# Reordering the last groups of a hybrid decoder layer: projections of p, the turn of x1, and the buffers of split weights

## The chip, the cores and the metric

The kernel runs on one core of a Trainium2 chip. The metric is the device time of one execution in microseconds; the time before is the median of three runs. A profiled execution beside them gives the trace: every instruction of the five engines (TensorE is PE, its weight loads PEld, VectorE is DVE, ScalarE is ACT, GpSimdE is POOL) and the transfers that SyncE (SP) and ACT issue.

## The reference, cut to what matters

One layer with 256 tokens and a width of 2048. All arithmetic is float32.

```python
h = rmsnorm(x, norm_mix_g)
u = h @ w_in                       # 2048 x 12288, ten fields
ya = b * causal_dwconv3(c * xa, conv_w) * silu(za)
yb = rmsnorm_per_head(hgrn2(silu(q), f, iv)) * hg_norm_g * silu(og)
m = sigmoid(ga) * (ya @ w_a_out) + sigmoid(gb) * (yb @ w_b_out)
x = x + m @ w_o                    # this x is called x1 below
gate = sigmoid(rmsnorm(x, ple_norm_g) @ w_ple_gate)
x = x + gate * (p @ w_ple_proj)    # p is 256 x 256
out = rmsnorm(x, final_norm_g)
```

The change concerns the last four lines.

## The kernel before

**Products.** Each float32 operand is split into a high and a low part, and each product is three matmuls: high with high, high with low, low with high (`product`, L834 to L836). The stationary operand is a slice of 128 tokens by 128 features, the moving one 512 columns of weights. A weight matrix is cut into *groups* of 512 output columns, and a group into *chunks* of 256 input features. A chunk is 12 matmuls: two slices of 128 features, two halves of the tokens, three products. Each group fills two PSUM banks, one for each half of the tokens.

**The order of the groups** is the list `groups`: 24 of w_in with those of w_a and w_b between them, then O0 to O3 (w_o, eight chunks each), then PP0, PG0, PP1, PG1, PP2, PG2, PP3, PG3. PP is the projection of p (w_pp, one chunk), PG the gate (w_pg, eight chunks). Chunk c of PG needs features 256 c to 256 c + 255 of x1, so chunks 6 and 7 of each PG group need the quarter that O3 makes. PG3 is written apart, after the loop: it runs over its eight chunks three times (first half of the tokens with 512 columns, then the second half with 256 columns, twice), keeps its eight split pairs throughout, and its results go straight into the final norm.

**Weights** come in loads of two chunks (1 MB; those of w_pp have one chunk) into three raw buffers, issued by SP in order (`load`, L105; w_pp at L103). `split` (L118 and L119) makes a pair of each chunk: ACT copies the high part `whi`, DVE subtracts and writes the low part `wlo`. Pairs up to the second chunk of PG3 take four buffers in turn; the last six chunks of PG3 have six buffers of their own, in the pool `late`, which is opened at PP0 in the place of m. A pair's buffer is free when PE has done its chunk, a raw buffer when DVE has split both of its chunks. `ahead` says how far ahead of PE's chunk splits are written: three chunks, rising to eight over the first chunks of PG2:

```python
return LEAD + min(max(pos - (last_group - 8), 0), 5)
```

**Epilogues** are generators: each `advance()`, once for every chunk, runs the next piece of each that is active. `step` ties a piece behind the latest split on ACT and on DVE (`issue_after`). A scheduler then orders each engine's instructions from what is written and from its own estimates; on the chip every engine works through its list in that order. The epilogues that matter here:

- `ep_o` (after O0 to O3): DVE adds the two banks to x (L584), ACT squares for the norm (L585) and copies into another order (L591), then `turned` writes to DRAM with four transfers (L191) and reads back with one (L193), and after a lag of three pieces DVE transposes (L197). `put` then makes the high part `xh` on ACT (L155) and the low part `xl` on DVE (L156), four pieces each.
- `ep_pp` (after PP): ACT copies the two banks to `pw` (L608).
- `ep_pg` (after PG0 to PG2): ACT's sigmoid reads the two banks (L618), DVE multiplies by `pw` and adds to x (L621, L622), ACT squares (L623), POOL multiplies by the final gain (L630).

**PSUM.** The groups' banks are four, given in turn, so a group's two banks are those of the group before last; PG3 takes one bank for each of its three passes. PE can start a group only when the readers of the banks' earlier contents are done.

Of the kernel before, what the change touches and what calls it, by code (L numbers as in the profile page):

```python
# [11 lines left out]
AF = mybir.ActivationFunctionType  # L12
# [5 lines left out]
NT = T // P  # L18
# [5 lines left out]
CW = 512  # L24
# [20 lines left out]
def hybrid_kernel(ctx, tc, xT, x, pT, prm, gfin, masks, w_in, w_a, w_b, w_o, w_pg, w_pp, out):  # L45
    nc = tc.nc

    const = ctx.enter_context(tc.tile_pool(name="const", bufs=1))
    wp = ctx.enter_context(tc.tile_pool(name="wp", bufs=1))
# [6 lines left out]
    pools, closers = {}, {}  # L56

    def open_pool(name, side):
        closers[name] = ExitStack()
        pools[name] = closers[name].enter_context(  # L60
            tc.tile_pool(name=name, bufs=1, side=side, reuse_waits="tile")
        )

    def close_pool(name):
        closers.pop(name).close()
        del pools[name]
# [3 lines left out]
    state = {"tmp": "tmp1"}  # L70
# [3 lines left out]
    def nm(s):  # L74
        uid[0] += 1
        return f"{s}_{uid[0]}"

    def t4(tag="t4", bufs=None):
        bufs = bufs or {"tmp1": 8, "tmp2": 5, "tmp3": 5}[state["tmp"]]
        return pools[state["tmp"]].tile([P, 1024], F32, tag=tag, bufs=bufs, name=nm(tag))  # L80
# [4 lines left out]
    def sc(n, tag="sc", bufs=12):  # L85
        return small.tile([P, n], F32, tag=tag, bufs=bufs, name=nm(tag))
# [21 lines left out]
    def split(pos, halves=(0, 1)):  # L108
        w, g, c = stream[pos]
        src = load(pos)[:, c % 2, :]  # L110
        pool, n = (pools["late"], 6) if pos >= last_group + 2 else (wp, 4)
        if pos not in parts:
            parts[pos] = tuple(
                pool.tile([P, 2 * CW], F32R, tag=tag, bufs=n, name=nm(tag)) for tag in ("whi", "wlo")
            )
        hi, lo = parts[pos]
        s = slice(halves[0] * CW, (halves[-1] + 1) * CW)
        a = nc.scalar.activation(out=hi[:, s], in_=src[:, s], func=AF.Copy)  # L118
        v = nc.vector.tensor_tensor(  # L119
            out=lo[:, s], in0=src[:, s], in1=hi[:, s].bitcast(F32), op=ALU.subtract  # L120
        )
        state["splits"] = (a.ins, v.ins)
# [18 lines left out]
    def gain(base, k):  # L141
        return prm_t[:, base + k : base + k + 1]
# [28 lines left out]
    def blocks(ap):  # L171

        return ap.rearrange("p (c b e) -> p c b e", b=4, e=32)

    def spread(ap, t):

        return ap.rearrange("p (b c t e) -> p t c b e", b=4, c=4, t=NT)[:, t]  # L180

    def turned(src, lag, dst=None):

        d = dram.tile([P, 4, T], F32, tag="turn", bufs=3, name=nm("turn"))
        to = d.rearrange("(b i) a x -> a i b x", b=4)
        for a in range(4):  # L190
            nc.sync.dma_start(out=to[a], in_=src[32 * a : 32 * a + 32, :].rearrange("i (b x) -> i b x", b=4))  # L191
        yield
        nc.sync.dma_start(out=src, in_=d.rearrange("p a x -> p (a x)"))  # L193
        for _ in range(lag):
            yield
        dst = t4() if dst is None else dst
        nc.vector.transpose(  # L197
            out=dst.rearrange("p (k a e) -> p a k e", a=4, e=32), in_=src.rearrange("p (a k e) -> p a k e", a=4, e=32)
        )
        return dst  # L200
# [377 lines left out]

    def ep_o(j, psum):
        xs = state["x"]  # L580
        src = t4()
        for t in range(NT):
            d = xs[:, t, j * CW : (j + 1) * CW]
            nc.vector.tensor_tensor(out=d, in0=d, in1=psum[t], op=ALU.add)  # L584
            nc.scalar.activation(  # L585
                out=src[:, t * CW : (t + 1) * CW], in_=d, func=AF.Square,
                accum_out=state["ss2"][:, t * 4 + j : t * 4 + j + 1],
            )
        x1 = src
        for t in range(NT):  # L590
            nc.scalar.activation(  # L591
                out=spread(x1, t), in_=blocks(xs[:, t, j * CW : (j + 1) * CW]), func=AF.Copy
            )
        x1 = yield from turned(x1, 3)
        for c in range(4):
            put(state["x1T"], j * 4 + c, x1[:, c * T : (c + 1) * T], gain(PRM_GPLE, j * 4 + c))
        if j == 3:
            tot = sc(2, "tot2", 1)
            nc.vector.tensor_reduce(
                out=tot, in_=state["ss2"].rearrange("p (t j) -> p t j", t=NT),  # L600
                axis=mybir.AxisListType.X, op=ALU.add,
            )
            state["rstd2"] = rsqrt_of(tot, NT, D, "r2")
# [76 lines left out]
    groups = []  # L680
    for n, (kind, j) in enumerate(IN_ORDER):
        groups.append((kind, j, w_in, n, "hT"))
        if kind == "gb":
            groups.append(("A", j, w_a, j, "yaT"))
            groups.append(("B", j, w_b, j, "ybT"))
    groups += [("O", j, w_o, j, "mT") for j in range(4)]
    for j in range(4):
        groups.append(("PP", j, w_pp, j, "pT"))
        groups.append(("PG", j, w_pg, j, "x1T"))
    steps = []  # L690
    for gi, (kind, j, w, g, op) in enumerate(groups):
        for c in range(w.shape[2]):
            stream.append((w, g, c))
            steps.append((gi, c))

    last_group = len(steps) - w_pg.shape[2]
# [3 lines left out]
    LEAD, AHEAD = 3, 4  # L700
# [3 lines left out]
    for c in range(KT // 2):  # L704
        n = 2 * (c % 2)
        nc.sync.dma_start(
            out=xraw[c // 2].rearrange("p (k t) -> p k t", k=4)[:, n : n + 2, :],
            in_=xT[:, 2 * c : 2 * c + 2, :],
# [14 lines left out]
    def put_x(k):  # L723
        put(state["hT"], k, xraw[k // 4][:, (k % 4) * T : (k % 4 + 1) * T], gain(PRM_GMIX, k))
# [82 lines left out]
        state["ss3"] = sc(12, "ss3", 1)  # L807
        nc.gpsimd.memset(state["ss3"].rearrange("p (t j) -> p t j", t=NT)[:, :, 5:6], EPS)

    def step(e):  # L810

        a, v = state["splits"]
        with tc.issue_after(a), tc.issue_after(v):
            try:
                next(e)
            except StopIteration:
                active.remove(e)

    def advance():
        for e in list(active):  # L820
            step(e)

    def finish():
        while active:
            advance()

    def ahead(pos):

        return LEAD + min(max(pos - (last_group - 8), 0), 5)

    def product(psum, op, k, t, hi, lo, first, last):

# [2 lines left out]
        nc.tensor.matmul(psum, oh, lo, start=False, stop=False)  # L835
        nc.tensor.matmul(psum, ol, hi, start=False, stop=last)  # L836

    active = []
    psum = None
    done = 0  # L840
    for pos, (gi, c) in enumerate(steps[:last_group]):
        kind, j, w, g, opname = groups[gi]
        nch = w.shape[2]
        if kind == "PP" and j == 0:
            close_pool("m")
            open_pool("late", "left")
        while done < min(pos + 1 + ahead(pos), len(steps)):
            if done < 2:
                for i in range(2):
                    put_x(2 * done + i)  # L850
                    split(done, (i,))
            else:
                for k in range(2 * done, min(2 * done + 2, KT)):
                    put_x(k)
                split(done)
            done += 1
        if pos == 4:
            begin()
        if 0 <= pos - NORM < 4:
            add_squares(pos - NORM)  # L860
        if pos == NORM + 3:
            norm_of_x()
        if pos == NORM + 4:
            active.append(ep_f(0, waiting))
            step(active[-1])
            nc.sync.dma_start(out=mask_t, in_=masks)
        if c == 0:
            psum = [bank("g") for _ in range(NT)]
        hi, lo = parts.pop(pos)
        for i in range(2):  # L870
            k = 2 * c + i
            s = slice(i * CW, (i + 1) * CW)
            for t in range(NT):
                product(psum[t], state[opname], k, t, hi[:, s], lo[:, s], k == 0, k == 2 * nch - 1)

        for q in range(done, min(done + AHEAD, len(steps)) if pos >= FIRST else 0):
            load(q)
        if 0 <= pos - TOKENS < 4:
            load_tokens(pos - TOKENS)
        advance()  # L880
        if kind == "O" and j == 0 and c == nch - 3:
            finish()
            third_part()
        if kind == "O" and j > 0 and c == 1:
            residual(j)
        if kind == "O" and j in (1, 2) and c == 4:
            (load_p, load_gfin)[j - 1]()
        if c == nch - 1:
            if kind == "f" and j == 0:

                waiting = psum
                for n in ("yaT", "ybT"):
                    state[n] = operand(pools["branch"], n, DC // P)
            if kind == "ga" and j == 0:
                finish()
                second_part()
            if kind == "O" and j == 0:
                state["x1T"] = operand(big, "x", KT)
            if kind == "f" and j == 0:
                continue  # L900
            active.append(epilogues[kind](j, psum))
            step(active[-1])

# [1 line left out]
    for t, halves in ((0, (0, 1)), (1, (0,)), (1, (1,))):  # L907
        bk, n = bank("g"), CW // 2
# [91 lines left out]
```

## Time and profile before

| | before |
|---|---|
| median of 3 runs | 842.76 us (842.6 to 843.79) |
| profiled execution | 842.37 us |
| its span | 840.6 us |
| PE busy | 824.0 us, 98% of the span |
| DVE busy | 528.3 us, 63% |
| ACT busy | 435.4 us, 52% |
| mean granted TensorE clock | 0.995 |

The span runs from the first instruction of the program to the last; the execution's own time is 1.8 us longer. Matmuls overlap, each row of one lasting longer than the step to the next, so the step from start to start is what a matmul costs. A bracket at the end of a row gives the idle time of that engine before it, and who ended it.

### The profile page before, as it was taken

What the parts mean: (1) busy time and instruction counts of PE and PEld (TensorE: products, weight loads), DVE (VectorE), ACT (ScalarE), POOL (GpSimd) and SP (SyncE); (2) the same over time, 40 slices, a digit from 0 to 9 for tenths busy, and PEclk for the clock granted to TensorE, in tenths of its full rate; (3) what the DMA queues carried; (4) which work ended last, traced back from release to release, by engine and by line L of the source; (5) the groups of instructions that cost most, each with busy time, mean ns of one, the idle gap of its engine ahead of it and who ended that gap; (6) DMA issues with size and microseconds to landing.
All of it is one profiled execution on the core that took longest, in us unless ns stands there. A gap on an engine that the chain in (4) does not pass through costs nothing.

```text
span 840.6 us, 9805 instructions
## 1 busy us (share of the span) xinstructions
PE 824.0 (98%) x3752; PEld 683.3 (81%) x3752; DVE 528.3 (63%) x600; ACT 435.4 (52%) x563; POOL 91.5 (11%) x76
## 2 busy tenths in 40 slices
PE   8999999999999999999999999999999999999985
PEld 5888888888888888888888888888888888878865
DVE  7558687777674777877546446454555566655552
ACT  7566654545564654545544444444444555654543
POOL 1000153100000243100001001001001000002110
PEclk9999999999999999999999999999999999999998
DMA  9977555648775555458557557556556877865512
GB/s 335 367 252 254 181 195 176 225 151 288 254 234 187 191 198 190 161 197 283 188 191 244 200 200 241 191 191 228 204 197 225 292 261 255 305 225 177 205 70 101
DMA packets 39792, 183.01 MB, mean 218 GB/s; under 512 B 4544, under 2 KB 13760, under 8 KB 21824
## 3 DMA queue, kind: packets, MB, share of 16 engines
q1 hardware_dynamic: 39312, 181.81, 62.4%
q8 instruction: 29, 0.48, 0.2%
q10 hardware_dynamic: 432, 0.56, 0.2%
q14 instruction: 19, 0.16, 0.0%
HBM read 170.82 MB, written 11.53 MB: 217 GB/s over the span
## 4 chain that ended last, share of the span: by engine, by line
PE 94%; DMA 2%; issue 1%; ACT 1%; DVE 1%; SPq 0%; POOLq 0%; POOL 0%
PE g L836 31%; PE g L835 31%; PE g L834 31%; PE s L327 1%; DMA raw<-in_w_pg 1%; DMA raw<-in_w_in 1%; ACT whi L118 1%; DVE wlo L119 1%; PE s L436 0%; PE s L449 0%; PE s L448 0%; PE s L447 0%; ACT xs L659 0%; ACT t L642 0%; SPq L713 0%
## 5 line engine op out<-in xcount | busy, mean ns | idle before, releaser
L119 DVE TENSOR_TENSOR wlo<-raw,whi 128x1024 fp32r<-128x1024 f32 (+1 forms) x294 | 360.2, 1229 | 272.4 <-ACT whi L118 271.7
L118 ACT ACTIVATE whi<-raw 128x1024 fp32r<-128x1024 f32 (+1 forms) x294 | 308.9, 1053 | 353.2 <-PE g L836 314.2
L834 PE MATMUL g<-whi,xh 128*128 128x512 f32 (+1 forms) x912 | 352.9, 388 | 6.2 <-ACT t L618 3.4
L835 PE MATMUL g<-wlo,xh 128*128 128x512 f32 (+1 forms) x912 | 352.6, 387 | 0.0
L836 PE MATMUL g<-whi,xl 128*128 128x512 f32 (+1 forms) x912 | 352.0, 386 | 0.0
L834 PEld LDWEIGHTS g<-whi,xh 128*128 128x128 f32 x912 | 171.6, 188 | 42.0 <-ACT t L618 3.9
L835 PEld LDWEIGHTS g<-wlo,xh 128*128 128x128 f32 x912 | 171.7, 188 | 34.9 <-DVE wlo L119 1.2
L836 PEld LDWEIGHTS g<-whi,xl 128*128 128x128 f32 x912 | 171.7, 188 | 34.9 <-DVE xl L156 0.5
L835 PE MATMUL g<-wlo,mh 128*128 128x512 f32 x128 | 49.6, 389 | 0.0
L834 PE MATMUL g<-whi,mh 128*128 128x512 f32 x128 | 49.5, 389 | 0.0
L836 PE MATMUL g<-whi,ml 128*128 128x512 f32 x128 | 49.5, 389 | 0.0
L572 POOL TENSOR_TENSOR t<-ga,gb 128x512 f32<-128x512 f32 x8 | 14.1, 1789 | 249.1 <-DVE gb L568 249.1
L836 PEld LDWEIGHTS g<-whi,ml 128*128 128x128 f32 x128 | 24.0, 188 | 5.0
L834 PEld LDWEIGHTS g<-whi,mh 128*128 128x128 f32 x128 | 24.0, 188 | 5.0
L835 PEld LDWEIGHTS g<-wlo,mh 128*128 128x128 f32 x128 | 24.0, 188 | 4.9
L373 POOL TENSOR_TENSOR t<-b 128x512 f32<-128x512 f32 x10 | 20.8, 2085 | 65.3 <-DMA raw<-in_w_in 33.6
L355 POOL TENSOR_TENSOR X<-t,kT 128x256 f32<-128x256 f32 x12 | 14.1, 1173 | 99.4 <-ACT t L369 57.7
L834 PE MATMUL g<-whi,yaTh 128*128 128x512 f32 x64 | 24.9, 389 | 0.0
L835 PE MATMUL g<-wlo,yaTh 128*128 128x512 f32 x64 | 24.9, 389 | 0.0
L836 PE MATMUL g<-whi,yaTl 128*128 128x512 f32 x64 | 24.9, 389 | 0.0
L834 PE MATMUL g<-whi,ybTh 128*128 128x512 f32 x64 | 24.9, 389 | 0.0
L835 PE MATMUL g<-wlo,ybTh 128*128 128x512 f32 x64 | 24.9, 389 | 0.0
(148 smaller groups left out, 555.5 us busy)
## 6 DMA issues: line engine op xcount, KB each, us to landing
raw<-in_w_in SPq DMA_DIRECT2D x91, 1024.0 KB, 4.9
raw<-in_w_o SPq DMA_DIRECT2D x16, 1024.0 KB, 5.9
raw<-in_w_pg SPq DMA_DIRECT2D x16, 1024.0 KB, 4.8
turn<-t SPq DMA_DIRECT2D x72, 128.0 KB, 2.9
t<-turn SPq DMA_DIRECT2D x18, 512.0 KB, 4.9
raw<-in_w_a SPq DMA_DIRECT2D x8, 1024.0 KB, 4.9
raw<-in_w_b SPq DMA_DIRECT2D x8, 1024.0 KB, 5.0
raw<-in_w_in SPq DMA_DIRECT2D x9, 512.0 KB, 7.7
```

Source lines behind the costliest of these rows:

```text
L118: a = nc.scalar.activation(out=hi[:, s], in_=src[:, s], func=AF.Copy)
L119: v = nc.vector.tensor_tensor(out=lo[:, s], in0=src[:, s], in1=hi[:, s].bitcast(F32), op=ALU.subtract)
L327: nc.tensor.matmul(bk[:, s], X[:, 0, h, :], X[:, 1, h, :], start=True, stop=True)
L355: eng.tensor_tensor(out=xv[:, w, :, :, half, :], in0=ev[:, :, blk, :, half, :], in1=src[:, :, blk, :, half, :], op=ALU.mult,)
L373: nc.gpsimd.tensor_tensor(out=er, in0=br, in1=ref, op=ALU.subtract)
L572: nc.gpsimd.tensor_tensor(out=spread(m, t), in0=blocks(ga[:, s]), in1=blocks(gb[:, s]), op=ALU.add)
L834: nc.tensor.matmul(psum, oh, hi, start=first, stop=False)
L835: nc.tensor.matmul(psum, oh, lo, start=False, stop=False)
L836: nc.tensor.matmul(psum, ol, hi, start=False, stop=last)
```

## The change

It has three parts.

- **Groups.** PP0 and PP1 both stand before PG0, then PP2, PG1, PP3, PG2, PG3. For PP chunks `advance()` runs ahead of the loads instead of behind them.
- **x1.** `ep_o` copies each half right after its add, and writes the turn in its first piece; the squares go to the second piece, with a junk tile of their own, and the transpose comes one piece earlier. O3's first piece isn't tied behind the latest splits, and once the last split is written, none is.
- **Pairs.** From the fourth chunk of PG0 on, pairs take ten buffers in turn: six of `late`, then the four. `late` is opened at PG0. `ahead` rises from three by one for every four chunks, from PG1's second chunk on.

```diff
 def split(pos, halves=(0, 1)):
-        pool, n = (pools["late"], 6) if pos >= last_group + 2 else (wp, 4)
+        pool, n = (pools["late"], 6) if (pos - state.get("late", len(steps))) % 10 < 6 and "late" in state else (wp, 4)
...
     def ep_o(j, psum):
         xs = state["x"]
-        src = t4()
+        x1 = t4()
         for t in range(NT):
             d = xs[:, t, j * CW : (j + 1) * CW]
             nc.vector.tensor_tensor(out=d, in0=d, in1=psum[t], op=ALU.add)
+            nc.scalar.activation(out=spread(x1, t), in_=blocks(d), func=AF.Copy)
+        turn = turned(x1, 2)
+        next(turn)
+        yield
+        junk = t4()
+        next(turn)
+        for t in range(NT):
             nc.scalar.activation(
-                out=src[:, t * CW : (t + 1) * CW], in_=d, func=AF.Square,
+                out=junk[:, t * CW : (t + 1) * CW], in_=xs[:, t, j * CW : (j + 1) * CW], func=AF.Square,
                 accum_out=state["ss2"][:, t * 4 + j : t * 4 + j + 1],
             )
-        x1 = src
-        for t in range(NT):
-            nc.scalar.activation(
-                out=spread(x1, t), in_=blocks(xs[:, t, j * CW : (j + 1) * CW]), func=AF.Copy
-            )
-        x1 = yield from turned(x1, 3)
+        yield
+        x1 = yield from turn
...
     groups += [("O", j, w_o, j, "mT") for j in range(4)]
+    groups.append(("PP", 0, w_pp, 0, "pT"))
     for j in range(4):
-        groups.append(("PP", j, w_pp, j, "pT"))
+        if j < 3:
+            groups.append(("PP", j + 1, w_pp, j + 1, "pT"))
         groups.append(("PG", j, w_pg, j, "x1T"))
...
-    def step(e):
-
-        a, v = state["splits"]
-        with tc.issue_after(a), tc.issue_after(v):
+    def step(e, free=False):
+
+        with ExitStack() as order:
+            for i in state["splits"] if done < len(steps) and not free else ():
+                order.enter_context(tc.issue_after(i))
...
-        return LEAD + min(max(pos - (last_group - 8), 0), 5)
+        return LEAD + min(max(pos - (last_group - 20), 0) // 4, 5)
...
-        if kind == "PP" and j == 0:
+        if kind == "PG" and j == 0 and c == 0:
             close_pool("m")
             open_pool("late", "left")
+            state["late"] = done
...
+        if kind == "PP":
+            advance()
         for q in range(done, min(done + AHEAD, len(steps)) if pos >= FIRST else 0):
             load(q)
         if 0 <= pos - TOKENS < 4:
             load_tokens(pos - TOKENS)
-        advance()
+        if kind != "PP":
+            advance()
...
-            step(active[-1])
+            step(active[-1], kind == "O" and j == 3)
```

## The prediction

> **What bounds the kernel now.** I read the page first (span, engine shares, the chain that ended last), then sums by stage, then the chain and the engines' time lines where the sums show TensorE short. The page:
>
> ```profile
> span 840.6 us, 9805 instructions
> PE 824.0 (98%) x3752; PEld 683.3 (81%) x3752; DVE 528.3 (63%) x600; ACT 435.4 (52%) x563; POOL 91.5 (11%) x76
> raw<-in_w_pg SPq DMA_DIRECT2D x16, 1024.0 KB, 4.8
> turn<-t SPq DMA_DIRECT2D x72, 128.0 KB, 2.9
> t<-turn SPq DMA_DIRECT2D x18, 512.0 KB, 4.9
> ```
>
> The last three rows are DMA issues, with the median us from issue to landing. PE is busy 98% of the span, so TensorE's list sets the end, so an edit is worth what it takes out of that list's holes. The sums by stage (stretch, length; busy time and instructions of PE, PEld, DVE, ACT, POOL; granted clock, DMA share, GB/s) show where the holes after the w_o groups are:
>
> ```profile
> 725.40:746.90 21.50, 21.50 (x96) 17.80 (x95) 11.65 (x13) 11.64 (x16) 0.71 (x1) 1.00 0.75 249
> 746.90:750.50 3.60, 2.01 (x8) 1.01 (x8) 3.26 (x6) 2.65 (x5) 0.00 (x0) 1.00 0.40 164
> 803.50:811.20 7.70, 4.26 (x13) 3.05 (x12) 5.19 (x7) 5.46 (x10) 0.53 (x1) 0.78 0.19 81
> ```
>
> Two holes: near 747, and near 804 with a clock of 0.78 in it. Their matmul rows (start, duration, engine, line; the bracket is idle time and its releaser):
>
> ```profile
> 724.52 0.39 PE L836 MATMUL g<-whi,ml 128*128 128x512 f32 x1
> 725.20 0.39 PE L836 MATMUL g<-whi,ml 128*128 128x512 f32 x1
> 725.43 0.39 PE L834 MATMUL g<-whi,ph 128*128 128x512 f32 x1
> ...
> 746.96 0.39 PE L836 MATMUL g<-whi,pl 128*128 128x512 f32 x1
> 748.90 0.50 PE L834 MATMUL g<-whi,xh 128*128 128x512 f32 x1 [1.54 <-ACT xh L155]
> 749.24 0.40 PE L835 MATMUL g<-wlo,xh 128*128 128x512 f32 x1
> 749.71 0.40 PE L835 MATMUL g<-wlo,xh 128*128 128x512 f32 x1
> 750.15 0.72 PE L836 MATMUL g<-whi,xl 128*128 128x512 f32 x2
> ...
> 803.57 0.39 PE L836 MATMUL g<-whi,pl 128*128 128x512 f32 x1
> 807.40 0.64 PE L834 MATMUL g<-whi,xh 128*128 128x512 f32 x1 [3.44 <-ACT t L618]
> 811.14 0.39 PE L834 MATMUL g<-whi,xh 128*128 128x512 f32 x1
> ```
>
> Undisturbed, three matmuls take 0.68 us (724.52 to 725.20), 0.227 each; a chunk is 12, so 2.72. The first hole: 746.96 to 748.90 is 1.94, less 0.23, is 1.71; the next ones are long by 0.11 (748.90 to 749.24), 0.21 (749.71 to 750.15) and 0.10 (0.72 for two, against 0.62): 2.1 us. The second: 3.83 less 0.23, 3.6 us. After it nine steps take 3.74 (807.40 to 811.14) instead of 2.04: 1.7 us of low clock. **Together 7.4 us**, and the change has nothing else to win: the stretch before the first hole is busy for all of its 21.50 us.
>
> The second hole's chain (start, duration, what), read upwards from the matmul at 807.40:
>
> ```profile
> 790.40 1.07 ACT whi L118
> ...
> 792.74 4.67 DMA raw<-in_w_pg
> 797.43 1.07 ACT whi L118
> 798.52 2.37 DVE wlo L119 x2
> 800.91 4.78 DMA raw<-in_w_pg
> 805.71 1.06 ACT whi L118
> 806.77 0.58 ACT t L618
> ```
>
> PG3 needs a PSUM bank that PG2 filled, so PG2's sigmoid (L618). It stands on ACT behind splits that run up to eight chunks ahead; with four pairs for everything before, these start only at 790.4, and then two loads in series sit between.
>
> **The change, part by part.** All times below are on this profile's clock; O3, the last w_o group, hands over at 725.43. I take the order of each engine's instructions from the changed program as built, and durations from rows.
>
> *The projections.* PP0 and PP1 now stand before PG0, PP2 before PG1 and PP3 before PG2, the same matmuls: no cost. PSUM gives banks in turn, two of two, so PG0, PG1, PG2 now take the banks of PP0, PG0, PG1, and PG3 first those of PP3. So PG3 no longer waits for PG2's sigmoid, but PG0 waits for the copies of PP0 (ep_pp), which before had a whole group's time.
>
> *x1's last quarter.* Before, its transpose came at 746.91 and then xh and xl, for which PE waited:
>
> ```profile
> 718.56 1.23 DVE L119 TENSOR_TENSOR wlo<-raw,whi 128x1024 fp32r<-128x1024 f32 x1 [1.49 <-ACT whi L118]
> 719.71 1.24 DVE L197 STREAM_TRANSPOSE t<-t 128x1024 f32<-128x1024 f32 x1
> 721.52 1.69 DVE L156 SCALAR_TENSOR_TENSOR xl<-t,prm_t,xh 128x256 fp32r<-128x256 f32 x4 [0.58 <-ACT xh L155]
> 725.95 1.28 DVE L584 TENSOR_TENSOR xs<-xs,g 128x512 f32<-128x512 f32 x2
> 746.91 1.24 DVE L197 STREAM_TRANSPOSE t<-t 128x1024 f32<-128x1024 f32 x1
> ...
> 725.68 1.06 ACT L118 ACTIVATE whi<-raw 128x1024 fp32r<-128x1024 f32 x1 [1.09 <-PE g L836]
> 726.66 0.63 ACT L585 ACTIVATE t<-xs 128x512 f32<-128x512 f32 x1
> 727.29 0.62 ACT L585 ACTIVATE t<-xs 128x512 f32<-128x512 f32 x1
> 727.91 0.58 ACT L608 ACTIVATE pw<-g 128x512 f32<-128x512 f32 x1
> 728.38 1.14 ACT L591 ACTIVATE t<-xs 128x512 f32<-128x512 f32 x2
> ...
> 729.55 2.57 SPq L191 DMA_DIRECT2D turn<-t  x4
> 736.65 0.33 SPq L193 DMA_DIRECT2D t<-turn  x1
> ```
>
> In the changed lists DVE reads, from the row at 718.56 on: PP0's wlo, transpose, xl once, add of O3's first half, xl three times, **PP1's wlo, then the add of the second half**. O3's first half ends at 724.52 + 0.39 = 724.91; PE's end frees ACT after 0.09 (725.20 + 0.39 to 725.68); with 0.2 for DVE, my estimate from that, the add starts at 725.1. Start to start: add 0.63 (1.28 for two), three xl of 0.42, wlo 1.15 (718.56 to 719.71), add 0.65: done at 728.8. PP1 needs these banks and that wlo: its matmuls come at 728.15 (first half) and 728.83 (second), so PP1 just gets through.
>
> ACT reads: copy of the first half, PG0c0's split, copy of the second half, PG0c1's split, two squares, **then PP0's two copies**. From 728.8: copy 0.53, split 0.97 (725.68 to 726.66), squares 1.25 (726.66 to 727.91), copy 0.58: PP0's first bank is read at 732.15. PE is through PP0 and PP1 at 725.43 + 5.44 = 730.87. **PG0 starts at 732.2: a new wait of 1.3 us.** Its second bank is free by 732.6, before its second half wants it (732.9). This wait is not in the trace of before. Bounds: zero, if ACT and DVE gain 1.3 us on these rows; 3.4 if the copies also slip past another split and add. A gain below zero is excluded, as PE does the same matmuls. I take 1.3.
>
> The Trainium skill (TensorE: Matmul & The Clock Gate, "Architectural detail") has ACT and DVE take instructions in strict order, which speaks against this part: a ready copy cannot overtake. The trace agrees (L618 at 806.77 behind the split at 805.71).
>
> The turn's four writes need both copies, 729.4, so they go out as at 729.55 before, the last at 732, and land 2.9 later. The read-back has only PG0c6's load ahead of it on SP (its raw buffer is free at 731.6, with PG0c1's wlo), so it starts near 735 instead of 736.65 and lands 4.9 later, at 740. The transpose stands after PG0c6's wlo: by then the new pairs let DVE run ahead, about 741; xh by 743.4, xl by 745.6. PG0c6 wants them at 732.2 + 6 x 2.72 = 748.5. **The hole of 2.1 us goes**, with about 3 us to spare. On SP the writes of the earlier quarters move ahead of one w_o load each; four issues take 2.57, and that load's chunk is wanted six chunks (16.3 us) later, load 4.8 and split 2.3 included: nothing. Squares, junk tile and one step less change no count on the path.
>
> *Ten pairs.* From PG0c3 on, six more pairs serve in turn with the four. Three raw buffers go round in 4.8 (load) + 1.06 + 2 x 1.15 = 8.2 us for six chunks, PE needs 16.3 for these: the splits get ahead until pairs or a sigmoid hold them. PG0's sigmoid stands behind PG1c2's split (raw buffer free with PG0c7's wlo at 742.8, load 4.8, split: 748.7) and waits for PG0's end at 754; PG1 wants the bank at 756.6. PG1's sigmoid stands behind PG2c7's. After PG0's sigmoids (755.4) ACT and DVE do the rest of PG0's epilogue and PG1c3 to c5 by 762.0; this frees the raw buffer of PG2c0 and c1: load to 766.8, their splits to 770.3, load of PG2c6 and c7 to 775.1, split to 777.2. PG1's end is 778.4, so the sigmoid isn't late; margin 2.7 us. PG3c6 and the rest are split by 799.8, PG3 starts at 802.9 in PP3's banks, nothing waits. **Hole of 3.6 and low clock of 1.7 go.**
>
> The clock: 1.54 idle left the next steps at 0.23 to 0.34, 3.44 idle was followed by 0.43 steps. So the new 1.3 should cost no clock. The Trainium skill (same page, "What's actually happening") says the half clock comes after an idle window of about 3.4 us and lasts about as long; the trace agrees (3.44 idle, low until 811.14).
>
> **Sum.** 2.1 + 3.6 + 1.7 - 1.3 = 6.1 us. The profiled execution took 842.37 (span 840.6), the median is 842.76: 836.3 and 836.7. I forecast 836.5. The stretch after the last matmul stays as it is.
>
> **Rivals.**
> A. The bank wait at PG0 is absorbed, no hole left: 842.76 - 7.4 = 835.3. For it: the estimate hangs on sums of small rows. Against: eight instructions in a fixed order. 0.12.
> B. The bank wait is longer, 2.5 to 3.4 us, and at its end starts the low clock (1.7): 837.9 to 840.5. For it: DVE and ACT wait for one another three times there. 0.17.
> C. PG3 still waits as before, since the loads and not the pairs held it: only 2.1 - 1.3 is won, 842.0, within 0.2%. Against: the chain starts with a split at 790.40 released by PE, not by a load. 0.04.
> D. Slower: PG1's sigmoid starves behind PG2c7's split, and PE stands before PG2 with a clock drop. Two loads in series lie there with a margin of 2.7 us. To undo 6.1 us, 4.4 of wait and 1.7 of clock are needed, so the two loads must take 8.3 us each. At 9.5 each: wait 6.7, clock 1.7, 844.9 us. For it: such times occur in this kernel's crowded start (next row). Against: the w_pg loads have 4.8 in the median. 0.05.
>
> ```profile
> raw<-in_w_in SPq DMA_DIRECT2D x9, 512.0 KB, 7.7
> ```
>
> **Numbers.** Forecast 0.62 (its own range 835.5 to 837.8, the wait at 0.3 to 2.4), A 0.12, B 0.17, C 0.04, D 0.05. Faster 0.91, same 0.04, slower 0.05; 0.2% is 1.7 us, about what a measurement of this kernel can tell from no change. The range, 834.9 to 838.9, takes A, the forecast and the lower half of B.
>
> **What would show it.** Right: no idle before PG0's seventh chunk and before PG3, no 0.43 steps after it, clock 1.00 in both, and one idle of about 1.3 before the first matmul of whi,xh, released by ACT pw. Wrong: that idle at zero or beyond 3, an idle at PG1 or PG2 released by a sigmoid or a load, or a hole inside the w_o groups.

## The result and the profile after

The changed kernel took 836.98 us (median; 836.68 to 836.98), the kernel before 842.83 in the same comparison (842.6 to 843.79): a ratio of 0.9926, 95% interval 0.9915 to 0.9938. In a second comparison it was 836.33 against 842.84, 0.9921 (0.9908 to 0.9933). The profiled execution took 836.98.

In the code after the change, `product` is L842 to L844, `split` L119 and L120; in `ep_o` the add is L585, the copy into another order L586, the square L593; `pw` is copied at L612, the sigmoid is L622, the transpose L198, `xh` and `xl` are written at L156 and L157. First the page of the changed kernel (its span and the share of each engine):

```profile
span 835.2 us, 9807 instructions
...
PE 822.8 (99%) x3752; PEld 684.1 (82%) x3752; DVE 529.3 (63%) x600; ACT 434.2 (52%) x563; POOL 91.9 (11%) x76
```

The sums by stage, from O3's end to behind the place of the second hole (columns as in the prediction):

```profile
725.40:731.70 6.30, 6.30 (x30) 5.14 (x28) 5.25 (x8) 3.71 (x7) 0.00 (x0) 1.00 0.29 79
731.70:735.00 3.30, 2.43 (x11) 1.75 (x10) 1.38 (x2) 3.30 (x8) 0.00 (x0) 1.00 1.10 348
735.00:803.50 68.50, 68.50 (x304) 56.75 (x303) 48.01 (x47) 39.95 (x53) 9.34 (x5) 1.00 0.60 222
803.50:811.20 7.70, 7.70 (x35) 6.38 (x35) 2.58 (x4) 2.49 (x6) 2.53 (x2) 1.00 0.00 0
```

PE is now busy for the whole of the third and fourth stretch, at a granted clock of 1.00; only the second has idle time. PE's time line shows which matmul that is:

```profile
726.19 0.39 PE L844 MATMUL g<-whi,ml 128*128 128x512 f32 x1
...
731.66 0.39 PE L844 MATMUL g<-whi,pl 128*128 128x512 f32 x1
732.91 0.50 PE L842 MATMUL g<-whi,xh 128*128 128x512 f32 x1 [0.87 <-ACT pw L612]
733.25 0.40 PE L843 MATMUL g<-wlo,xh 128*128 128x512 f32 x1
...
749.37 0.39 PE L842 MATMUL g<-whi,xh 128*128 128x512 f32 x1
...
803.54 0.39 PE L844 MATMUL g<-whi,xl 128*128 128x512 f32 x1
803.76 0.39 PE L842 MATMUL g<-whi,xh 128*128 128x512 f32 x1
...
826.04 0.28 PE L844 MATMUL g<-whi,xl 128*128 128x256 f32 x1
```

PG0 starts at 732.91 behind the `pw` copy: 1.25 from start to start less the undisturbed 0.23 is 1.02, and the next step is long by 0.11 (0.34): 1.1 us. Its seventh chunk, from 749.37, and PG3, at 803.76, have no bracket, so no idle time: both holes are gone. What made PE wait is seen on ACT:

```profile
729.58 0.63 ACT L586 ACTIVATE t<-xs 128x512 f32<-128x512 f32 x1 [1.34 <-DVE xs L585]
730.11 1.04 ACT L119 ACTIVATE whi<-raw 128x1024 fp32r<-128x1024 f32 x1
731.06 0.61 ACT L593 ACTIVATE t<-xs 128x512 f32<-128x512 f32 x1
...
732.29 1.06 ACT L612 ACTIVATE pw<-g 128x512 f32<-128x512 f32 x2
```

ACT waits 1.34 for DVE's second add, then takes the copy, a split and two squares before it reads PP0's banks, while PE is already through PP1.

To compare profiles without what differs at their starts, take the stretch from the start of the last w_o matmul to the start of the last matmul: 99.85 us here (826.04 - 726.19), 106.20 before (831.40 - 725.20). That is 6.35 less. The spans differ by 5.4 only, since O3 ended 0.99 later in this execution; the last section returns to that.

### The profile page after: what moved, and what is told of

The parts are those of the page before. It is cut to its first block, busy times and chain, and to the rows that moved or that the text cites. A ratio compares the mean times of both kernels' runs of the same rounds, so it can differ in the third digit from the quotient of the medians.

```text
span 835.2 us, 9807 instructions
## 1 busy us (share of the span) xinstructions
PE 822.8 (99%) x3752; PEld 684.1 (82%) x3752; DVE 529.3 (63%) x600; ACT 434.2 (52%) x563; POOL 91.9 (11%) x76
## 4 chain that ended last, share of the span: by engine, by line
PE 96%; issue 1%; ACT 1%; DVE 0%; DMA 0%; POOLq 0%; POOL 0%; DVEq 0%; ACTq 0%
PE g L842 31%; PE g L844 31%; PE g L843 31%; PE s L328 1%; DMA prm_t<-in_prm 0%; PE s L437 0%; PE s L450 0%; PE s L449 0%; PE s L448 0%; ACT whi L119 0%; ACT xs L663 0%; ACT t L593 0%; DVE wlo L120 0%; DVE xl L157 0%; ACT t L646 0%
## 5 line engine op out<-in xcount | busy, mean ns | idle before, releaser
L120 DVE TENSOR_TENSOR wlo<-raw,whi 128x1024 fp32r<-128x1024 f32 (+1 forms) x294 | 361.5, 1234 | 258.5 <-ACT whi L119 257.6
L119 ACT ACTIVATE whi<-raw 128x1024 fp32r<-128x1024 f32 (+1 forms) x294 | 308.1, 1053 | 340.8 <-PE g L844 292.3
L842 PE MATMUL g<-whi,xh 128*128 128x512 f32 (+1 forms) x912 | 353.0, 388 | 2.0 <-ACT whi L119 1.2
L844 PE MATMUL g<-whi,xl 128*128 128x512 f32 (+1 forms) x912 | 352.0, 386 | 0.0
L842 PEld LDWEIGHTS g<-whi,xh 128*128 128x128 f32 x912 | 171.8, 189 | 37.2 <-ACT whi L119 2.1
L844 PEld LDWEIGHTS g<-whi,xl 128*128 128x128 f32 x912 | 171.7, 188 | 34.4
L842 PE MATMUL g<-whi,mh 128*128 128x512 f32 x128 | 49.5, 389 | 0.0
L844 PE MATMUL g<-whi,ml 128*128 128x512 f32 x128 | 49.5, 389 | 0.0
L842 PEld LDWEIGHTS g<-whi,mh 128*128 128x128 f32 x128 | 24.0, 188 | 5.0
L844 PEld LDWEIGHTS g<-whi,ml 128*128 128x128 f32 x128 | 24.0, 188 | 4.9
L842 PE MATMUL g<-whi,yaTh 128*128 128x512 f32 x64 | 24.9, 389 | 0.0
L844 PE MATMUL g<-whi,yaTl 128*128 128x512 f32 x64 | 24.9, 389 | 0.0
L842 PE MATMUL g<-whi,ybTh 128*128 128x512 f32 x64 | 24.9, 389 | 0.0
```

The costliest lines, as they stand in the source:

```text
L120: v = nc.vector.tensor_tensor(out=lo[:, s], in0=src[:, s], in1=hi[:, s].bitcast(F32), op=ALU.subtract)
L842: nc.tensor.matmul(psum, oh, hi, start=first, stop=False)
```

## The experiments

Each of these kernels ran five rounds against the kernel before, whose medians were 842.56 to 843.49; the comparisons were on different chips. "Stretch" is the one just defined, from one profiled execution of each; the two kernels that were profiled twice repeat it to 0.05. "Lost behind O3" is PE's idle time there and its steps at low clock, over the undisturbed step, from the matmul rows.

| kernel | median us | ratio to before, 95% | stretch us | lost behind O3, us |
|---|---|---|---|---|
| before | 842.83 | 1 | 106.20 | 7.4 |
| after | 836.98 | 0.9926 (0.9915 to 0.9938) | 99.85 | 1.1 |
| e1, without the pairs | 836.0 | 0.9924 (0.991 to 0.9937) | 99.85 | 1.1 |
| e2, without the groups | 835.7 | 0.9918 (0.9905 to 0.9932) | 98.88 | 0.1 |
| e3, without x1 | 836.53 | 0.9926 (0.9913 to 0.9938) | 99.46 | 0.7 |
| e5, the pairs alone | 835.02 | 0.9905 (0.989 to 0.992) | 98.66 | 0 |
| e6, the groups alone | 836.52 | 0.9923 (0.991 to 0.9936) | 99.42 | 0.7 |
| e7, x1 alone | 840.65 | 0.9971 (0.9962 to 0.998) | 103.97 | 5.2 |
| e4, after with O3's squares later | 835.46 | 0.9915 (0.99 to 0.993) | 98.68 | 0 |
| e8, after with four squares | 839.27 | 0.9949 (0.9935 to 0.9963) | 102.64 | 3.9 |
| e9, after, a square between the copies | 836.64 | 0.9926 (0.9913 to 0.994) | 99.89 | 1.2 |
| e12, after, three squares first | 837.18 | 0.9935 (0.992 to 0.9949) | 100.47 | 1.8 |
| e10, after again | 836.33 | 0.9921 (0.9908 to 0.9933) | 99.90 | 1.2 |
| e11, the pairs alone again | 834.88 | 0.9906 (0.9892 to 0.9919) | 98.66 | 0 |

**Which part closes which hole: one part undone.** The first three kernels are the changed one with one part put back. Two details aren't split here as "The change" splits them. The pieces freed once the last split is written go with the pairs: e1 and e7 are without them, e3 and e5 have them. They change nothing in e5 or in the changed kernel, which are the same programs without them. And `late` is opened at PG0 in all of these kernels; in e6 and e7, where that is no part of the pairs, it changes the order of no engine's instructions.

e1, the pairs and `ahead` as before:

```diff
-        pool, n = (pools["late"], 6) if (pos - state.get("late", len(steps))) % 10 < 6 and "late" in state else (wp, 4)
+        pool, n = (pools["late"], 6) if pos >= last_group + 2 else (wp, 4)
...
-            for i in state["splits"] if done < len(steps) and not free else ():
+            for i in state["splits"] if not free else ():
...
-        return LEAD + min(max(pos - (last_group - 20), 0) // 4, 5)
+        return LEAD + min(max(pos - (last_group - 8), 0), 5)
```

> The changed kernel with the old buffers of split pairs (four, and six for the end of PG3) and the old rise of the lookahead. My theory: the hole before PG3 needed two things together, PG2's bank and splits that start late; the new order of groups gives PG3 the banks of PP3, so it stays closed without the ten pairs: about 837.0 us, with the 1.1 us wait at PG0 as in the changed kernel. Rival (the pairs closed it): PE stands again 3.6 us before PG3 and pays 1.7 us of low clock, about 842.3 us.

Its wait before PG0 and the stretch at PG3:

```profile
731.89 0.50 PE L842 MATMUL g<-whi,xh 128*128 128x512 f32 x1 [0.87 <-ACT pw L612]
```

```profile
803.50:811.20 7.70, 7.70 (x36) 6.38 (x35) 4.40 (x6) 3.04 (x7) 2.54 (x2) 1.00 0.00 1
```

The stretch is the changed kernel's to 0.01 us. With PG3 in PP3's banks the second hole stays closed without a single added pair, so the pairs are not needed for it, and they add nothing beside the other two parts.

e2, the groups as before:

```diff
-    groups.append(("PP", 0, w_pp, 0, "pT"))
     for j in range(4):
-        if j < 3:
-            groups.append(("PP", j + 1, w_pp, j + 1, "pT"))
+        groups.append(("PP", j, w_pp, j, "pT"))
...
-        if kind == "PP":
-            advance()
...
-        if kind != "PP":
-            advance()
+        advance()
```

> The changed kernel with the old order of groups (PP0 PG0 PP1 PG1 PP2 PG2 PP3 PG3). My theory: PG0 gets the banks of O3 again, which DVE's adds free at 728 or so, so the 1.1 us wait at PG0 goes; the earlier turn still closes the hole at PG0's seventh chunk, and the ten pairs close that before PG3 though PG2's sigmoid still frees its bank: about 835.5 us. Rival (the order of groups and its banks closed the second hole): 3.6 and 1.7 us come back, about 840.8 us.

As the theory said: no wait before PG0 (the two banks are not PP0's there), both holes closed, 98.88. Of the changed kernel's three parts the groups are the one whose removal gains most, 0.97 us of the stretch; e3 gains 0.39, e1 nothing.

e3, `ep_o` as before (its squares and copies too, not shown here):

```diff
...
-        turn = turned(x1, 2)
-        next(turn)
...
-        x1 = yield from turn
+        x1 = yield from turned(x1, 3)
...
-            step(active[-1], kind == "O" and j == 3)
+            step(active[-1])
```

> The changed kernel with the old epilogue of O0 to O3 (squares ahead of the copies, transpose one piece later, O3's first piece tied behind the splits). My theory: the hole at PG0's seventh chunk is back with 2 to 4 us (copies, turn and xh stand behind more splits), the 1.1 us wait at PG0 is smaller or gone since PP0's copies come ahead of the squares: 838 to 840 us. Rival (two projections ahead of PG0 give x1 time enough, and the turn's place does not matter): no hole there, about 835.8 us.

This theory was wrong. The first hole did not come back; what is lost is 0.7 us, at the starts of two groups. DVE's transpose in e3, and on PE's time line the second of these two starts:

```profile
744.28 1.24 DVE L198 STREAM_TRANSPOSE t<-t 128x1024 f32<-128x1024 f32 x1
```

```profile
755.55 0.50 PE L839 MATMUL g<-whi,xh 128*128 128x512 f32 x1 [0.16 <-ACT t L619]
```

Counted from the start of PP0 (725.00 here, 725.43 before), the transpose comes 2.2 us earlier than in the kernel before (746.91), although nothing in `ep_o` is moved. So the earlier turn isn't the only thing that closes the first hole.

**One part alone.** The next three are the kernel before with one part added.

e5, the pairs:

```diff
-        pool, n = (pools["late"], 6) if pos >= last_group + 2 else (wp, 4)
+        pool, n = (pools["late"], 6) if (pos - state.get("late", len(steps))) % 10 < 6 and "late" in state else (wp, 4)
...
-    def step(e):
-
-        a, v = state["splits"]
-        with tc.issue_after(a), tc.issue_after(v):
+    def step(e, free=False):
+
+        with ExitStack() as order:
+            for i in state["splits"] if done < len(steps) and not free else ():
+                order.enter_context(tc.issue_after(i))
...
-        return LEAD + min(max(pos - (last_group - 8), 0), 5)
+        return LEAD + min(max(pos - (last_group - 20), 0) // 4, 5)
...
-        if kind == "PP" and j == 0:
+        if kind == "PG" and j == 0 and c == 0:
             close_pool("m")
             open_pool("late", "left")
+            state["late"] = done
```

> The kernel before with the ten pairs and the slower rise of the lookahead alone. My theory: the hole before PG3 and its low clock close (5.3 us), the hole at PG0's seventh chunk stays or grows by up to 2 us, since xh now stands behind splits that run further ahead: 837.5 to 839.5 us. Rival (pairs do not close it without the new banks): 842.8 us or more.

Half right: the hole before PG3 went, but so did the first one. The sums around PG3's start (801.71 in e5), then DVE and PE at the first hole (there `product` is L837 to L839):

```profile
799.00:805.00 6.00, 6.00 (x28) 4.99 (x27) 2.58 (x4) 3.19 (x8) 2.54 (x2) 1.00 0.01 1
```

```profile
743.26 1.24 DVE L198 STREAM_TRANSPOSE t<-t 128x1024 f32<-128x1024 f32 x1
745.52 1.66 DVE L157 SCALAR_TENSOR_TENSOR xl<-t,prm_t,xh 128x256 fp32r<-128x256 f32 x4
```

```profile
747.09 0.39 PE L839 MATMUL g<-whi,pl 128*128 128x512 f32 x1
747.31 0.39 PE L837 MATMUL g<-whi,xh 128*128 128x512 f32 x1
```

With four pairs, DVE's list stood behind splits that waited for PE to free a pair; with ten these go ahead, and the transpose in the same list moves from 746.91 to 743.26. ACT's split ahead of the transpose, in the kernel before and in e5, shows what it waited for:

```profile
744.67 1.06 ACT L118 ACTIVATE whi<-raw 128x1024 fp32r<-128x1024 f32 x1 [1.66 <-PE g L836]
```

```profile
741.02 2.01 ACT L119 ACTIVATE whi<-raw 128x1024 fp32r<-128x1024 f32 x2 [3.27 <-DMA raw<-in_w_pg]
```

PE goes from PP1's last product to PG0's seventh chunk without a pause.

e6, the groups:

```diff
+    groups.append(("PP", 0, w_pp, 0, "pT"))
     for j in range(4):
-        groups.append(("PP", j, w_pp, j, "pT"))
+        if j < 3:
+            groups.append(("PP", j + 1, w_pp, j + 1, "pT"))
...
+        if kind == "PP":
+            advance()
...
-        advance()
+        if kind != "PP":
+            advance()
```

> The kernel before with the new order of groups alone. My theory: PG3 takes the banks of PP3, and the 5.3 us before it close without any new buffer; the hole at PG0's seventh chunk stays at about 2 us: about 837.5 us. Rival (the four pairs are what holds PG3): 842.8 us.

The hole before PG3 closed, as expected: PE has no idle time there. The hole expected at PG0's seventh chunk was not there either; 0.7 us was lost instead of 2. DVE, then PE (`product` is L839 to L841):

```profile
746.96 1.24 DVE L198 STREAM_TRANSPOSE t<-t 128x1024 f32<-128x1024 f32 x1
...
749.68 1.66 DVE L157 SCALAR_TENSOR_TENSOR xl<-t,prm_t,xh 128x256 fp32r<-128x256 f32 x4
```

```profile
747.25 0.39 PE L839 MATMUL g<-whi,ph 128*128 128x512 f32 x1
...
749.97 0.39 PE L839 MATMUL g<-whi,xh 128*128 128x512 f32 x1
```

The transpose is as late as before, but PE has one more projection in front of PG0's seventh chunk: its 12 matmuls from 747.25 to 749.97 lie where the hole was. (PE's order is the scheduler's too: it puts a projection right in front of that chunk before and in e3, e5 and e6, but not in the changed kernel.) The new wait before PG0 isn't here either: it needs the moved squares too. In the profile it takes groups and x1 together (after, e1), and is in neither alone (e6, e7).

e7, x1 (the `ep_o` of the change, three lines of which are shown, and the freed step of O3):

```diff
...
+        turn = turned(x1, 2)
+        next(turn)
...
-        x1 = yield from turned(x1, 3)
+        x1 = yield from turn
...
+            step(active[-1], kind == "O" and j == 3)
```

> The kernel before with the new epilogue of O0 to O3 alone. My theory: the hole at PG0's seventh chunk closes (2.1 us), the one before PG3 stays: about 840.7 us. Rival (the turn needs the pairs' freedom to come earlier, as DVE and ACT stand behind splits): no gain, 842.8 us.

As said: the first hole is closed, the second remains. PE's rows of e7 there:

```profile
801.77 0.39 PE L842 MATMUL g<-whi,pl 128*128 128x512 f32 x1
805.42 0.50 PE L840 MATMUL g<-whi,xh 128*128 128x512 f32 x1 [3.26 <-ACT t L622]
805.76 0.40 PE L841 MATMUL g<-wlo,xh 128*128 128x512 f32 x1
...
806.69 0.59 PE L842 MATMUL g<-whi,xl 128*128 128x512 f32 x1
807.08 0.63 PE L840 MATMUL g<-whi,xh 128*128 128x512 f32 x1
807.50 0.63 PE L841 MATMUL g<-wlo,xh 128*128 128x512 f32 x1
```

After 3.26 us of idle time the steps are first full speed (0.23 to 0.34) for 1.3 us and only then 0.42.

**The new wait.** e4 is the changed kernel with O3's squares one piece later:

```diff
-        junk = t4()
         next(turn)
+        if j == 3:
+            yield
+        junk = t4()
...
-        yield
+        if j < 3:
+            yield
```

> The changed kernel with the two squares of O3 one piece later, so that on ACT the two copies of PP0 come ahead of them; same instructions. My theory: the wait at PG0 (1.0 us of idle and 0.1 in the next step) hangs on these copies, which come 1.25 us earlier: no idle, about 835.8 us, below both kernels. Rival (PG0 waits for something that stands ahead of the squares as well, DVE's second add or a split): the wait stays, about 837.0 us.

ACT and PE of e4 (its `pw` copies are L615, `product` L845 to L847):

```profile
730.97 1.07 ACT L615 ACTIVATE pw<-g 128x512 f32<-128x512 f32 x2
```

```profile
731.78 0.39 PE L845 MATMUL g<-whi,xh 128*128 128x512 f32 x1
```

The copies come right behind the split, PG0 starts with no pause, the stretch is 98.68. With the squares out of the way there is no wait left.

e8 writes O3's squares twice (the second time the same values again), to lengthen the wait:

```diff
-        for t in range(NT):
+        for t in (0, 1, 0, 1) if j == 3 else range(NT):
```

> The changed kernel with the two squares of O3 done twice (the same result written again). My theory: PP0's copies stand behind them on ACT, so the wait at PG0 grows by the 1.25 us that two squares take: about 838.2 us, and the clock stays full as the idle time stays under 3.4 us. Rival (the squares are hidden and PG0 waits for something else): 837.0 us.

```profile
731.16 0.39 PE L844 MATMUL g<-whi,pl 128*128 128x512 f32 x1
733.67 0.80 PE L842 MATMUL g<-whi,xh 128*128 128x512 f32 x1 [2.12 <-ACT pw L612]
734.26 0.63 PE L843 MATMUL g<-wlo,xh 128*128 128x512 f32 x1
```

The wait grew as expected, from 1.0 to 2.3 us, but 2.12 us of idle time was already followed by 0.43 steps up to 736.8; I had expected full speed below 3.4. The six executions took 839.25 to 839.61 four times, 837.8 and 837.41: it looks as if two of them kept the clock, but only the first kind was profiled.

e9 and e12 have three squares, to find where between 1.0 and 2.1 the clock starts to suffer. In e9 the second half is squared twice:

```diff
-        for t in range(NT):
+        for t in (0, 1, 1) if j == 3 else range(NT):
```

> The after kernel with one more of O3's squares (three instead of two, the second half squared twice), ahead of the second copy of PP0's banks. The wait before PG0 was 1.03 us with two squares and 2.28 with four; three should make it about 1.65, if each square on ACT's list adds 0.63 to the step. Theory one, the half clock needs an idle time of about 2 us or more: no 0.43 steps behind the wait in any execution, and every time within 1 us of after's plus 0.6, so about 837.6. Theory two, the half clock depends on where the idle time falls against a window that runs on its own: some executions show the drop also with 1.65 us, so the times fall into two groups about 1.6 us apart, the upper near 839.

That missed its aim: ACT's list put the third square between the two copies, and the wait did not grow. ACT and PE of e9:

```profile
731.81 0.57 ACT L612 ACTIVATE pw<-g 128x512 f32<-128x512 f32 x1
732.28 0.62 ACT L593 ACTIVATE t<-xs 128x512 f32<-128x512 f32 x1
```

```profile
732.43 0.50 PE L842 MATMUL g<-whi,xh 128*128 128x512 f32 x1 [0.90 <-ACT pw L612]
```

So only the first of the two copies is on PE's path; the second has at least a square's time to spare. In e12 the first half is squared twice, and all three squares stand ahead of both copies:

```diff
-        for t in range(NT):
+        for t in (0, 0, 1) if j == 3 else range(NT):
```

> The after kernel with three of O3's squares (the first half squared twice), all three ahead of the first copy of PP0's banks; with three squares placed around the first copy the wait stayed at 1.06 us, so only the first copy is on TensorE's path. Theory one, the half clock needs an idle time over 2 us: the wait is 1.68 us (1.06 and one square of 0.62), no 0.43 steps in any execution, all times within 0.5 us of 836.9. Theory two, it depends on where the idle time falls against a window that runs on its own: the drop shows in some executions, and the times fall into two groups about 1.6 us apart, the upper near 838.5.

```profile
730.97 0.39 PE L844 MATMUL g<-whi,pl 128*128 128x512 f32 x1
732.85 0.50 PE L842 MATMUL g<-whi,xh 128*128 128x512 f32 x1 [1.49 <-ACT pw L612]
733.18 0.39 PE L843 MATMUL g<-wlo,xh 128*128 128x512 f32 x1
```

A wait of 1.65 with full speed behind it, and all five executions within 836.57 to 837.49. Here 1.49 us idle cost no clock, 2.12 did.

**After and the pairs alone, side by side.** The two kernels ran again on one chip, unchanged (e10, e11).

> The after kernel once more, for a direct comparison on one chip with the ten pairs alone. Theory: 0.9926 of before, its profile with the one wait of about 1.0 us before PG0 and no other idle time over 0.3 us behind O3, and a start that takes 725.0 to 726.4 us up to O3's end, whatever the kernel.

> The ten pairs alone once more. Theory, these do all that the change does and leave out the wait that groups and x1 make together: faster than after by that wait, 1.1 us, and with no idle time over 0.3 us behind O3. Rival, the 1.96 us between them in separate comparisons were those of different chips and of the start: no difference beyond 0.3 us.

The pairs alone are the faster: 834.69 to 835.35 against 835.71 to 836.53, with no overlap; 1.45 us between the medians, 1.24 between the stretches. Nearly all of the latter is the one wait, 1.17 in e10. The page of e11's sums by stage, over PG0's start:

```profile
725.40:735.00 9.60, 9.60 (x44) 7.96 (x43) 6.97 (x9) 8.93 (x14) 0.00 (x0) 1.00 0.75 220
```

## Why the prediction was right, step by step

It forecast 836.5 us (834.9 to 838.9); measured were 836.98 and 836.33.

- **The bound.** PE's holes behind O3 were all there was to win. Over the twelve experiments the stretch follows what is lost there: 98.66 with nothing lost, 106.20 with 7.4.
- **The first hole (2.1 us) goes.** Right in size and place. The transpose was put at about 741, on a clock on which O3 ended 0.99 earlier; measured 742.47. `xl` was done at 747.5 and wanted at 749.37, so 1.9 us were to spare where I had about 3. But the reason was too narrow. I gave the hole to x1's earlier turn, with the pairs as a help to the transpose, and expected it back without that turn (e3, e5, e6); it didn't come back in any of them. Three things close it, each by itself: the earlier turn (e7), the splits that no longer hold DVE's list (e5), and one more projection in front of the seventh chunk (e6). The changed kernel doesn't have this third one: there the scheduler starts the chunk at 749.37 and puts a quarter of PP2 into it at 750.27, the rest behind PG0. The prediction had listed the move of PP2 as "the same matmuls: no cost", and missed that it can also be cover.
- **The hole before PG3 (3.6) and its low clock (1.7) go.** Right. The two reasons given for it, PP3's banks and the ten pairs, are again each enough (e6 and e1 for the banks, e5 for the pairs). e7, with neither, keeps it. Rival C, that the loads hold PG3, is out: e5 keeps the old banks and changes the pairs and their lead, and the hole is gone. The pairs and the slower rise of `ahead` were not tried apart.
- **The new wait (1.3 us).** Right in place, releaser and nearly in size: 1.1. With the start 0.99 later, the 732.2 becomes 733.2; PG0 started at 732.91. The order written down from the lists (copy, split, copy, split, two squares, then `pw`) is what the trace shows. e4, with the squares behind those copies, loses it and takes 835.46, about what rival A gave for no wait at all (835.3).
- **No clock lost by it.** True at 0.87 us idle, but the argument behind it had no support between 1.54 and 3.44. Rival B's price was real at a shorter wait than it assumed: 2.12 us in e8 cost low clock as well.
- **The margin at PG2.** Right in the mechanism, but the size depends on the execution. I took two loads in series at 4.8 us each and had 2.7 us left. ACT's rows in the changed kernel, then the sigmoids of the same kernel in its second profile (e10):

```profile
778.72 2.01 ACT L119 ACTIVATE whi<-raw 128x1024 fp32r<-128x1024 f32 x2 [1.84 <-DMA raw<-in_w_pg]
780.64 1.25 ACT L622 ACTIVATE t<-g,r2r 128x512 f32<-128x512 f32 x2
```

```profile
778.51 1.24 ACT L622 ACTIVATE t<-g,r2r 128x512 f32<-128x512 f32 x2
```

PG1's sigmoid does stand behind PG2c7's split, as said, and ACT did wait for that load. PE begins PG2 at 782.00, and the first of the two sigmoids is done at about 781.3: 0.7 us were left. In e10 PE begins PG2 at 781.55, the first sigmoid is done at about 779.2, and 2.4 us were left. The two loads in series, of PG2's first and last two chunks, took 4.85 and 6.27 us in the first profile, 4.73 and 4.71 in the second; why the 6.27, isn't shown. Where the loads are slow, rival D was nearer than a chance of 0.05 says, and a kernel that loads a little later might meet it; that wasn't tried.
- **The sum.** 7.4 less 1.1 is 6.3, and the stretch shrank by 6.35; the forecast had 6.1. In time it was 5.85 (836.98 against 842.83) in the first comparison and 6.51 in the second (836.33 against 842.84); what lies between is in part the start, below.

The three parts don't add: alone they shorten the stretch by 2.2 us (e7), 6.8 (e6) and 7.5 (e5), all three together by 6.35. They close the same two holes, and two of them meet in a new wait.

## What to carry to other kernels

Where several edits aim at the same hole, undo and apply them one by one: here the pairs alone did all of it, and the full set was slower by the one wait that two of the edits made together. When a group's PSUM bank gets a new predecessor, look up who reads that predecessor's result and what stands ahead of that reader on its engine; a few squares there are on TensorE's path although their results are wanted only later. A chunk of independent matmuls placed in front of the one that waits can close a hole as an earlier operand does.

## What the runs showed of the hardware that I had not expected

**The low clock.** 1.49 us of idle time left full speed behind it (e12), 2.12 us did not (e8), and in e7 the low clock began 1.3 us after the pause of 3.26 had ended. The granted clock in the traces is 0.50 from 733.59 to 737.00 in e8, from 806.71 to 810.12 in e7 and from 807.61 to 811.02 before: 3.41 us each time, however long the pause was. The Trainium skill (TensorE: Matmul & The Clock Gate, "What's actually happening") has the half clock come after at least one idle window of about 3.4 us, and has that window run on its own, not restarted by the kernel. The late begin in e7 and the two kinds of time in e8 agree with a window that runs on its own; 3.4 us as the least idle time does not agree with 2.12, and the measurement decides. Where exactly the limit lies, and whether it moves with the window, is open.

**The start.** O3 ended between 725.0 and 726.4 in the profiles (start of the first projection), though PE's matmuls up to there are the same and, from 17 us on, no step between them is longer than 0.32 us in any profile. It goes with the first product. Here are the first matmuls of the changed kernel, then those of e12:

```profile
6.22 1.22 PE L842 MATMUL g<-whi,xh 128*128 128x512 f32 x2 [1.17 <-ACT whi L119]
7.24 0.63 PE L843 MATMUL g<-wlo,xh 128*128 128x512 f32 x1
```

```profile
5.89 0.73 PE L842 MATMUL g<-whi,xh 128*128 128x512 f32 x2 [0.84 <-ACT whi L119]
...
7.19 0.39 PE L843 MATMUL g<-wlo,xh 128*128 128x512 f32 x1
```

In the eight profiles in which the first product started at 5.79 to 5.91, the steps were at full speed from about 7; in the six in which it started at 5.93 to 6.22, they stayed at 0.43 until about 9.7 to 10.7. The last w_o matmul started at 724.8 to 725.5 in the first kind, at 725.7 to 726.2 in the second. The second kind so ends about 0.7 us later (means 725.2 and 725.9). That the later product causes the low clock isn't shown: the clock record of the first kind grants full speed from 4.1 to 5.5 us, ahead of the first product, that of the second only from 9.7 to 10.7. Both kinds occur among the kernels made from the changed one; whether it is chance of the execution or a property of a kernel, the runs don't settle. It is why differences under 1 us were read from the stretch and not from the time.
